# Sums of squares for the norms: transposed squares summed by VectorE in place of fp32 products with ones, with another table of turns

## The chip, the cores and the metric

The kernel runs on one core of a Trainium2 chip. The metric is the device time of one execution in microseconds; less is better. A core has five engines, each with its own instruction queue that is worked off in order: TensorE (PE; its weight loads are listed apart as PEld), VectorE (DVE), ScalarE (ACT), GpSimd (POOL) and SyncE (SP), which here issues nearly all transfers between HBM and SBUF. PE writes its results to PSUM, and the other engines read them there.

## The reference

One layer over 2048 tokens of width 1024: a normed input is multiplied by one wide weight, and its parts go to three branches (RWKV-7 with 8 heads of 64, sliding-window attention with 8 query and 2 key heads of 64, cross-attention into 256 memory tokens with 4 heads of 128), which are gated, merged and projected back. What the change touches are the norms per head, each of which needs the sum of squares of every token over the 64 or 128 channels of a head:

```python
def rms_norm(x, g):
    xf = x.astype(jnp.float32)
    y = xf * lax.rsqrt(jnp.mean(xf * xf, axis=-1, keepdims=True) + RMS_EPS)
    return (y * g.astype(jnp.float32)).astype(x.dtype)
...
kk = heads(k * k_k.astype(f32))
kk = kk / jnp.maximum(jnp.linalg.norm(kk, axis=-1, keepdims=True), L2_EPS)      # RWKV
...
q = rope(rms_norm(q.reshape(bsz, t, SW_HEADS, SW_HEAD_DIM), q_g), pos)          # window
k = rope(rms_norm(k.reshape(bsz, t, SW_KV_HEADS, SW_HEAD_DIM), k_g), pos)
...
q = rms_norm(q.reshape(bsz, t, X_HEADS, X_HEAD_DIM), xq_g)                      # cross
km = rms_norm(km.reshape(bsz, m, X_HEADS, X_HEAD_DIM), xk_g)
```

## The kernel before

**Tiling.** The tokens are worked through in four blocks of 512 (`TB`, the loop over `sb`). Activations stand channel by token: 128 partitions hold 128 channels, 512 columns hold tokens. Every large product is made from three products of split operands (`gemm3`, lines 462 to 464: high by high, low by high, high by low, in the type fp32r), 128 by 128 weights against 512 columns. These are called the dense products below. The small products (heads, transposes, chunk products of RWKV) are in plain fp32.

**Weights.** `wblock` (lines 440 to 448) fetches a weight block into the ring `whl` of nine buffers. In the first token block it loads the raw weight (443), ACT makes the high half (444), DVE the low half (445), and SP stores both halves to HBM (448). In the later blocks the stored halves are loaded (440), and neither ACT nor DVE has to do with them. A store on SP waits for line 445, and the loads behind it on SP wait with it.

**The sums of squares.** ACT squares a projection into `sq` (128 channels by 512 tokens). Since the channels stand on partitions, the sum over a head's channels is taken by PE: `tok_stat` (lines 509 to 512) multiplies, for each 128 tokens, the tile `sq` as the stationary operand with `bones` (two columns, each with ones for 64 channels) or `ones1` (one column of ones). The result, tokens by heads, is 128 by 1 or 2 numbers in PSUM per product. DVE copies the 2 to 8 columns to `st8` (lines 626, 953, 1014, 1050; in RWKV line 725 takes a maximum in place of the copy and line 726 a reciprocal). Outside RWKV, POOL raises them to the power -1/2 (`rpow`, lines 427 to 431). Where the factor has to be channel by token again, `bcast_T` has DVE widen it (523) and PE transpose it back (525).

Each token block has thirteen such sums of four tiles: one per RWKV pair of heads (723), one per cross head (951), one for the window keys (1012), one per pair of window query heads (1048). The memory keys have four of two tiles in the first block (624). In all that is 4 x 13 x 4 + 4 x 2 = 216 tile products. The PSUM tiles come from two rings of two banks, `rw` in RWKV and `as_` elsewhere.

**The order.** Within a token block the code is written as five streams, and a string of `TURNS` (one for the first block, one for the others) says which stream goes on at each turn: r for RWKV, a for both attentions, b and c for two merges, g for gates. That is the program order. `order` then lays all instructions out: `Step` gives each a cost, `lay_out` fills each engine's queue by rank, and `latest` sets the ranks anew from due times, in three passes. Each engine's queue is then fixed in that order. A change of a cost or of a turn therefore moves instructions on every engine.

Of the kernel before, what the change touches and what calls it, by code (L numbers as in the profile page):

```python
# [9 lines left out]
F32 = mybir.dt.float32  # L10
# [4 lines left out]
ALU = mybir.AluOpType  # L15
# [6 lines left out]
NRT = 6  # L22
PASSES = 3
TURNS = (
    "rararrarbaaaaaaaaaaraaaaarbaracarbaabaaarbrgrabrraaaaarabbbaaaarrraararccccgcgccrgrgrrgrrgrrgrrrrc",
    "rararaaaaraaaraaaaarbraabararaabbaraaaaacaararraabbrbgraaaaarraabbarraccrgcccgrcrgrgrgrcrgrrgrrrrc",
)
RING = 9
C = 64
# [24 lines left out]
class Step:  # L54
# [36 lines left out]
    def cost_PE(self):  # L91
        out, mov, w = self.writes[0], *self.reads[:2]
        n = self.n(out)
        self.tile = tuple(128 if r[3][0][1] > 64 else 64 if r[3][0][1] > 32 else 32 for r in (mov, out))
        self.dense = mov[5] == F32R
        if self.dense:
            self.busy = max(110, 13.5 + 0.417 * n)
        elif self.ins.is_transpose:
            self.busy = 109 if self.tile[0] == 128 else 63
        elif self.tile[1] == 128:  # L100
            self.busy = 223 + max(0, n - 128) * 1.7
        else:
            self.busy = 34 if self.tile[1] < 64 else max(58, 0.86 * n) if self.tile[0] > 64 else max(58, 0.48 * n)
        self.dur = max(270, self.busy + 160)
# [66 lines left out]
def lay_out(tc, todo):  # L171
# [50 lines left out]
    for s in todo:  # L222
        if not missing[s]:
            offer(s)
    tile, fp32, wires = (128, 128), False, 0
    for _ in todo:
        best = None
        for e, rs in ready.items():
            if rs:
                at = max(clock[e], min(rs.values()))  # L230
                if best is None or at < best[0]:
                    best = at, e
        at, e = best
        can = [s for s, t in ready[e].items() if t <= at]
        s = min(can, key=lambda s: s.rank)
        if e == "PE":
            s = min(can, key=lambda s: (fp32 and s.tile != tile, s.rank))
            if s.tile != tile:
                at += 95
            clock[e] = at + s.busy  # L240
            if s.dense and fp32:
                clock[e] += 95
            elif s.tile != tile and s.tile[1] < 128:
                clock[e] += 49
            tile, fp32 = s.tile, not s.dense
        else:
            clock[e] = at + s.busy
        s.end = at + s.dur
        if s.bytes:
            wires = s.end = max(wires, s.end) + s.bytes / 330  # L250
        del ready[e][s]
        orders[e].append(s)
        again = set()
        for name in s.opens:
            tag = source[name]
            tags[tag].free.pop(0)
            heads[tag] += 1
            again.add(tag)
        for name in {r[0] for r in s.reads + s.writes}:
            if e not in last[name] or last[name][e].end < s.end:  # L260
                last[name][e] = s
            left[name] -= 1
            if not left[name] and source[name] in tags:
                tags[source[name]].free.append(name)
                again.add(source[name])
        for a in s.after:
            missing[a] -= 1
            if not missing[a]:
                offer(a)
        if again:  # L270
            for a in [a for rs in (parked, *ready.values()) for a in rs if any(source[n] in again for n in a.opens)]:
                offer(a)
# [45 lines left out]
def build(tc, A, nsb=4):  # L318
# [27 lines left out]
    def rw_ps():  # L346
        return ps.tile([128, 512], F32, name="rw", bufs=2)

    def s_ps():
        return ps.tile([128, 512], F32, name="as_", bufs=2)  # L350
# [155 lines left out]
        return o  # L506


    def tok_stat(sq, nh, ntile, out):
        rhs = bones if nh == 2 else ones1  # L510
        for i in range(ntile):
            PE.matmul(out[:, i * nh:(i + 1) * nh], sq[:, i * 128:(i + 1) * 128], rhs, start=True, stop=True)

    bones2 = cp.tile([128, 128], F32R, name="bones2")
    V.tensor_copy(bones2.rearrange("p (a b) -> p a b", b=64), bones.unsqueeze(2).to_broadcast([128, 2, 64]))
    ones1 = cp.tile([128, 1], F32, name="ones1")
    V.memset(ones1, 1.0)

    def bcast_T(out, st, nh, ntile):

# [89 lines left out]
    def mem_kv(mT):  # L610
# [9 lines left out]
            kgs[h] = sq, kg  # L620

        def stats(h):
            st = s_ps()
            tok_stat(kgs[h][0], 1, 2, st)
            rs = xp.tile([128, 8], F32, name="st8", bufs=2)
            V.tensor_copy(rs[:, :2], st[:, :2])
            rpow(rs[:, :2], rs[:, :2], EPS, 1.0 / 128)
            sts[h] = rs

# [63 lines left out]
    def rwkv_prep(p, sb, hT, lwla, group):  # L693
# [25 lines left out]
        yield  # L719
        sq = tmp()  # L720
        S.activation(sq, k, AF.Square, scale=pcol("k_k", p))
        st = rw_ps()
        tok_stat(sq, 2, 4, st)
        rs = xp.tile([128, 8], F32, name="st8", bufs=2)
        V.tensor_scalar(rs, st[:, :8], 1e-24, None, op0=ALU.max)
        V.reciprocal(rs, rs)
        rs2 = rw_ps()
        bcast_T(rs2, rs, 2, 4)
# [209 lines left out]
    def cross_head(h, sb, hT, yh, yl):  # L938
# [8 lines left out]
        sq = g2()  # L947
        S.activation(sq, o, AF.Square)
        yield
        st = s_ps()  # L950
        tok_stat(sq, 1, 4, st)
        rs = xp.tile([128, 8], F32, name="st8", bufs=2)
        V.tensor_copy(rs[:, :4], st[:, :4])  # L953
        rpow(rs[:, :4], rs[:, :4], 128 * EPS)
        mx = xp.tile([128, 8], F32, name="mx", bufs=2)
        sps = []
# [43 lines left out]
    def swa_kv(sb, hT):  # L1000
        o = slice(sb * TB, (sb + 1) * TB)
        if sb:
            G.tensor_copy(kH[:, :, :128], kH[:, :, TB:])
            G.tensor_copy(kL[:, :, :128], kL[:, :, TB:])
            G.tensor_copy(vt[:, 0], vt[:, 4])
        kp = proj(B_SK, hT)
        sq = g2()
        S.activation(sq, kp, AF.Square)
        kg = g2()
        S.activation(kg, kp, AF.Copy, scale=pcol("k_g"))  # L1010
        st = s_ps()
        tok_stat(sq, 2, 4, st)
        rs = xp.tile([128, 8], F32, name="st8", bufs=2)
        V.tensor_copy(rs, st[:, :8])
        rpow(rs, rs, EPS, 1.0 / 64)
        yield
        bc = s_ps()
        bcast_T(bc, rs, 2, 4)
        V.tensor_tensor(kg, kg, bc, op=ALU.mult)
        rope(kg, kg)  # L1020
        for g, h in enumerate((EV, OD)):
            for to in (h, EV if g else OD):
                S.activation(kH[to, g, 128:], kg[h], AF.Copy)
                V.tensor_tensor(kL[to, g, 128:], kg[h], kH[h, g, 128:].bitcast(F32), op=ALU.subtract)
        vp = proj(B_SV, hT)
        vs = g2()
        S.activation(vs, vp, AF.Copy)
        yield
        pt = s_ps()
        for i in range(4):  # L1030
            PE.transpose(pt[:, i * 128:(i + 1) * 128], vs[:, i * 128:(i + 1) * 128], ident)
        S.activation(vt[:, 1:].rearrange("p a b -> p (a b)"), pt, AF.Copy)

    def swa_pair(j, sb, hT, yh, yl):
# [9 lines left out]
            S.activation(q[h], qg[h], AF.Copy)  # L1044
            V.tensor_tensor(q[l], qg[h], q[h].bitcast(F32), op=ALU.subtract)
        yield
        st = s_ps()
        tok_stat(sq, 2, 4, st)
        rs = xp.tile([128, 8], F32, name="st8", bufs=2)
        V.tensor_copy(rs, st[:, :8])  # L1050
        rpow(rs, rs, 64 * EPS)
        g = j // 2
        mx = xp.tile([128, 4, 4], F32, name="mxs", bufs=2)
# [233 lines left out]
```

## Time and profile before

| | |
|---|---|
| median of 3 runs | 2307.17 us (2304.47 to 2309.24) |
| the profiled execution | 2305.93 us, its span 2304.2 us |
| DVE busy | 1436.1 us, 62% of the span |
| ACT, POOL busy | 840.3 us (36%), 218.1 us (9%) |
| DMA queues | 487.84 MB moved, mean 212 GB/s |
| records of line 512 (216 fp32 products) | two each, 432 |

The span runs from the first to the last instruction of the profiled execution; what lies around it is 1.7 us. The page gives busy times by engine, the span in 40 slices, the chain of work that ended last, and groups of instructions; the trace behind it answers for single lines, waits and windows. Matmuls overlap, so the duration of one (some 0.4 us for 512 columns) is longer than the distance from one start to the next, and it is the distances that add up.

### The profile page before, as it was taken

The numbers are of one execution on the slowest core, as the hardware profiler recorded it, in microseconds if no ns is written. First come the engines' busy times: TensorE is split into PE (matmuls) and PEld (weight loads), VectorE is DVE, ScalarE is ACT, GpSimd is POOL, SyncE is SP. The second block draws the span as 40 slices with busy tenths as digits, with TensorE's granted clock in tenths as the row PEclk, the third lists the DMA queues.
The fourth block names the chain that finished last, engine by engine and source line by source line (L and its number), as shares of the span: only waits on it lengthen the run. The fifth ranks groups of instructions, "written<-read, shape, count | busy, mean of one in ns | idle before, by whom it ended". The sixth has DMA issues, their size and how long they took to land.

```text
span 2304.2 us, 38725 instructions
## 1 busy us (share of the span) xinstructions
PE 2264.8 (98%) x14304; PEld 1857.4 (81%) x14304; DVE 1436.1 (62%) x4429; ACT 840.3 (36%) x1805; POOL 218.1 (9%) x297
## 2 busy tenths in 40 slices
PE   7999999999999999999999999999999999999999
PEld 6788888867788888887888888887788888888787
DVE  6698787637457866633627686762453777765252
ACT  5465545316334253311513343421232435241030
POOL 2001001021000000101101000101200000000210
PEclk9999999999999999999999999999999999999999
DMA  7777777777865555466674555556666554556665
GB/s 240 252 259 241 257 243 253 269 238 272 310 234 185 170 161 189 162 209 242 228 251 155 191 170 166 178 171 228 223 240 221 170 173 156 177 162 206 221 214 181
DMA packets 218077, 487.84 MB, mean 212 GB/s; under 512 B 19616, under 2 KB 81440, under 8 KB 217888
## 3 DMA queue, kind: packets, MB, share of 16 engines
q1 hardware_dynamic: 205216, 462.28, 60.0%
q10 hardware_dynamic: 12672, 23.07, 2.9%
q8 instruction: 114, 1.87, 0.3%
q14 instruction: 75, 0.61, 0.1%
HBM read 357.88 MB, written 127.40 MB: 211 GB/s over the span
## 4 chain that ended last, share of the span: by engine, by line
PE 86%; DVE 5%; DMA 4%; ACT 3%; issue 1%; POOL 0%; SPq 0%; ACTq 0%; POOLq 0%; DVEq 0%
PE mm L462 20%; PE mm L463 20%; PE mm L464 20%; PE rw L763 2%; DMA whl<-in_w_in 2%; PE mm L1144 1%; PE mm L1146 1%; PE mm L1145 1%; PE oo L1099 1%; PE oo L988 1%; PE rw L871 1%; PE rw L884 1%; PE rw L879 1%; ACT g L1079 1%; DVE whl L445 1%
## 5 line engine op out<-in xcount | busy, mean ns | idle before, releaser
L462 PE MATMUL mm<-hH,whl 128*128 128x512 f32 x1888 | 749.6, 397 | 7.8 <-ACT whl L444 7.3
L463 PE MATMUL mm<-hL,whl 128*128 128x512 f32 x1888 | 748.1, 396 | 0.0
L464 PE MATMUL mm<-hH,whl 128*128 128x512 f32 x1888 | 745.0, 395 | 0.0
L462 PEld LDWEIGHTS mm<-hH,whl 128*128 128x128 f32 x1888 | 355.4, 188 | 81.6 <-ACT whl L444 8.8
L463 PEld LDWEIGHTS mm<-hL,whl 128*128 128x128 f32 x1888 | 355.5, 188 | 73.3 <-issue 0.3
L464 PEld LDWEIGHTS mm<-hH,whl 128*128 128x128 f32 x1888 | 355.4, 188 | 72.0 <-DVE whl L445 1.3
L1110 ACT ACTIVATE g<-mm 128x512 f32<-128x512 f32 x96 | 57.5, 599 | 371.2 <-PE mm L464 371.0
L445 DVE TENSOR_TENSOR whl<-whl 128x512 fp32r<-128x512 f32 x174 | 121.0, 697 | 76.6 <-ACT whl L444 67.9
L444 ACT ACTIVATE whl<-whl 128x512 fp32r<-128x512 f32 x174 | 109.2, 629 | 153.8 <-DMA whl<-in_w_in 92.1
L782 DVE TENSOR_TENSOR ibc<-ibc,Yi 128x248 f32<-128x248 f32 (+30 forms) x496 | 143.8, 290 | 11.1
L462 PE MATMUL mm<-yh,whl 128*128 128x512 f32 x384 | 149.1, 390 | 1.6 <-ACT yh L932 0.8
L781 DVE STREAM_SHUFFLE ibc<-Nc 128x248 f32<-128x248 f32 (+30 forms) x496 | 150.4, 312 | 0.1
L463 PE MATMUL mm<-yl,whl 128*128 128x512 f32 x384 | 149.1, 390 | 0.1
L464 PE MATMUL mm<-yh,whl 128*128 128x512 f32 x384 | 149.1, 389 | 0.0
L783 DVE TENSOR_TENSOR Yi<-Yi,ibc 128x248 f32<-128x248 f32 (+30 forms) x496 | 140.2, 283 | 1.0
L1125 DVE SCALAR_TENSOR_TENSOR g<-g,mm 128x512 f32<-128x512 f32 x64 | 43.7, 684 | 91.0 <-PE mm L464 90.9
L1079 ACT ACTIVATE g<-g,mxs,st 128x256 f32<-128x256 f32 (+1 forms) x128 | 74.4, 584 | 43.6 <-DVE mxs L1072 23.4
L427 POOL TENSOR_SCALAR st<-st 128x4 f32<-128x4 f32 (+1 forms) x32 | 10.4, 324 | 810.1 <-DVE st L953 411.7
L462 PEld LDWEIGHTS mm<-yh,whl 128*128 128x128 f32 x384 | 72.0, 188 | 18.2 <-DVE g L1125 2.1
L463 PEld LDWEIGHTS mm<-yl,whl 128*128 128x128 f32 x384 | 72.1, 188 | 16.3 <-DVE yl L933 1.4
L464 PEld LDWEIGHTS mm<-yh,whl 128*128 128x128 f32 x384 | 72.1, 188 | 14.8
L877 POOL TENSOR_TENSOR SP<-Z,Pl 64x256 f32<-64x256 f32 x64 | 41.6, 650 | 305.7 <-DVE Z L890 204.4
(1735 smaller groups left out, 3495.4 us busy)
## 6 DMA issues: line engine op xcount, KB each, us to landing
whl<-k SPq DMA_DIRECT2D x474, 512.0 KB, 3.4
k<-whl SPq DMA_DIRECT2D x158, 512.0 KB, 3.3
whl<-f SPq DMA_DIRECT2D x128, 256.0 KB, 4.5
whl<-in_w_in SPq DMA_DIRECT2D x118, 256.0 KB, 3.6
f<-FT SPq DMA_DIRECT2D x48, 512.0 KB, 4.6
f<-FT SPq DMA_DIRECT2D x32, 256.0 KB, 4.1
g<-in_x ACTq DMA_DIRECT2D x32, 256.0 KB, 5.4
out<-g ACTq DMA_DIRECT2D x32, 256.0 KB, 4.1
```

What stands on the lines that cost most here:

```text
L444: S.activation(w[:, 0], raw, AF.Copy)
L445: V.tensor_tensor(w[:, 1], raw, w[:, 0].bitcast(F32), op=ALU.subtract)
L462: PE.matmul(out, lh, rh, start=i == 0, stop=False)
L463: PE.matmul(out, lh, rl, start=False, stop=False)
L464: PE.matmul(out, ll, rh, start=False, stop=i == n - 1)
L763: PE.matmul(g[:, c], BK[h, c0 + c], Q[h, c0 + c], start=True, stop=True)
L781: V.stream_shuffle(bc[:, :, :n], Nc[:, :, s + 1:], [s] * 32)
L782: V.tensor_tensor(bc[:, :, :n], bc[:, :, :n], Y[:, :, s:s + 1].to_broadcast([128, NC_, n]), op=ALU.mult)
L783: V.tensor_tensor(Y[:, :, s + 1:], Y[:, :, s + 1:], bc[:, :, :n], op=ALU.add)
L1079: S.activation(prs[b][:, i, m0:], prs[b][:, i, m0:], AF.Exp, scale=r2[:, b, i:i + 1], bias=mx[:, b, i:i + 1], accum_out=mx[:, b, 2 + i:3 + i])
L1110: S.activation(t, gp, AF.Tanh, scale=0.5)
L1125: V.scalar_tensor_tensor(g, g, 1.0, pp, op0=ALU.add, op1=ALU.mult)
```

## The change

`tok_stat` no longer multiplies with ones. PE transposes each 128 by 128 tile of squares into PSUM, so that tokens stand on partitions and channels on columns, and one `tensor_reduce` of DVE sums 64 or 128 columns each from PSUM straight into `st8`. The copies out of PSUM go; in RWKV the maximum stays, now on SBUF. `ones1` goes. The planner's cost of a transpose is set to 112 ns in place of 109, and what it adds to the first dense product after fp32 work is 30 ns after transposes alone, where it was 95 after any. Both turn strings are others.

```diff
@@ TURNS (the first of two strings)
-    "rararrarbaaaaaaaaaaraaaaarbaracarbaabaaarbrgrabrraaaaarabbbaaaarrraararccccgcgccrgrgrrgrrgrrgrrrrc",
+    "rrararaaaraaabaaaaaraaabrrraaaaabacbrbgaaaararrabrbaaabraabgaaararraararcccccccrggrrgrgrrgrrrrgrrc",
@@ cost_PE
         elif self.ins.is_transpose:
-            self.busy = 109 if self.tile[0] == 128 else 63
+            self.busy = 112 if self.tile[0] == 128 else 63
@@ lay_out
             if s.dense and fp32:
-                clock[e] += 95
+                clock[e] += fp32
...
-            tile, fp32 = s.tile, not s.dense
+            tile, fp32 = s.tile, 0 if s.dense else 30 if s.ins.is_transpose and fp32 < 95 else 95
@@ build
-    def tok_stat(sq, nh, ntile, out):
-        rhs = bones if nh == 2 else ones1
+    def tok_stat(sq, nh, ntile, pt):
+        rs = xp.tile([128, 8], F32, name="st8", bufs=2)
         for i in range(ntile):
-            PE.matmul(out[:, i * nh:(i + 1) * nh], sq[:, i * 128:(i + 1) * 128], rhs, start=True, stop=True)
+            PE.transpose(pt[:, i * 128:(i + 1) * 128], sq[:, i * 128:(i + 1) * 128], ident)
+        V.tensor_reduce(rs[:, :ntile * nh], pt[:, :ntile * 128].rearrange("p (a b) -> p a b", b=128 // nh), axis=AX.X, op=ALU.add)
+        return rs
@@ rwkv_prep
-        st = rw_ps()
-        tok_stat(sq, 2, 4, st)
-        rs = xp.tile([128, 8], F32, name="st8", bufs=2)
-        V.tensor_scalar(rs, st[:, :8], 1e-24, None, op0=ALU.max)
+        rs = tok_stat(sq, 2, 4, rw_ps())
+        V.tensor_scalar(rs, rs, 1e-24, None, op0=ALU.max)
@@ cross_head (mem_kv, swa_kv and swa_pair alike)
-        st = s_ps()
-        tok_stat(sq, 1, 4, st)
-        rs = xp.tile([128, 8], F32, name="st8", bufs=2)
-        V.tensor_copy(rs[:, :4], st[:, :4])
+        rs = tok_stat(sq, 1, 4, s_ps())
```

The order of the instructions moves on all engines. Three places show how; a number behind a name tells one buffer from another, and in the changed kernel the lines stand up to 14 earlier.

**PE, the first RWKV sum of the second token block.** Before, the four products with ones (L512, into `rw_6952`) stand between dense products, and seven dense products follow until the transposes of `bcast_T` (L525):

```order
L462 MATMUL mm_6915<-hH_6319,whl_6918 128x512
L463 MATMUL mm_6915<-hL_6320,whl_6918 128x512
L464 MATMUL mm_6915<-hH_6319,whl_6918 128x512
L512 MATMUL rw_6952<-c_bones_118,rt_6950 128x2 x4
L462 MATMUL mm_6981<-hH_6319,whl_6982 128x512
L463 MATMUL mm_6981<-hL_6320,whl_6982 128x512
```

In the changed kernel the transposes of the squares stand among those of a cross head (L976), with that head's products (L980) and three dense ones between them and L525:

```order
L976 MATMUL as__7099<-c_ident_96,g2_6926 128x128 x3
L512 MATMUL rw_6990<-c_ident_96,rt_6988 128x128 x4
L976 MATMUL as__7099<-c_ident_96,g2_6926 128x128
L976 MATMUL as__7110<-c_ident_96,g2_6929 128x128 x4
L462 MATMUL mm_7247<-hH_6321,whl_7248 128x512
L463 MATMUL mm_7247<-hL_6322,whl_7248 128x512
L464 MATMUL mm_7247<-hH_6321,whl_7248 128x512
L980 MATMUL oo_7098<-g2_7106,vm_6862 128x256 x2
L980 MATMUL oo_7098<-g2_7117,vm_6862 128x256 x2
L525 MATMUL rw_6999<-c_ident_96,rt_7000 128x128 x4
```

The sum has moved next to other transposes, and its work is now one of a row of transposes.

**PE, the sum for the window keys in the second token block** (L512 into `as__8061` before, `as__7979` now). Before, eleven more dense products follow the last row shown until the transposes L525 into `as__8196`:

```order
L462 MATMUL mm_8217<-hH_6319,whl_8218 128x512
L463 MATMUL mm_8217<-hL_6320,whl_8218 128x512
L512 MATMUL as__8061<-c_bones_118,g2_8057 128x2 x4
L464 MATMUL mm_8217<-hH_6319,whl_8218 128x512
L462 MATMUL mm_8217<-hH_6319,whl_8218 128x512
```

In the changed kernel chunk products of RWKV (L758, line 763 before) stand on both sides, and after the last row shown eight more dense products follow until L525 into `as__7988`:

```order
L758 MATMUL rw_8045<-FT_165 128x128 x4
L758 MATMUL rw_8046<-FT_165 128x128 x4
L512 MATMUL as__7979<-c_ident_96,g2_7975 128x128 x4
L462 MATMUL mm_8212<-hH_6321,whl_8213 128x512
L758 MATMUL rw_8057<-FT_165 128x128 x4
L758 MATMUL rw_8058<-FT_165 128x128 x4
L463 MATMUL mm_8212<-hL_6322,whl_8213 128x512
L464 MATMUL mm_8212<-hH_6321,whl_8213 128x512
```

So between sum and L525 stood 13 dense products, and now stand eleven and eight chunk products.

**DVE, the same place.** Before, the copy of the sums (L1014), one step of the rope tables (L559) and the widening copy (L523) follow each other:

```order
L556 CAST g2_7968<-g2_7974 128x512
L558 SCALAR_TENSOR_TENSOR g2_7963<-g2_7968,g2_7963 128x512 x4
L1014 COPY st8_8066<-as__8061 128x8
L559 TENSOR_SCALAR g2_7963<-g2_7963 128x512
L523 COPY rt_8197<-st8_8066 128x512
```

In the changed kernel the reduction (L513) stands where the copy stood, and four operations, two of them on the chunk products (L760), stand between it and the widening copy:

```order
L513 TENSOR_REDUCE st8_7980<-as__7979 128x8
L558 SCALAR_TENSOR_TENSOR g2_7847<-g2_7852,g2_7847 128x512
L760 TENSOR_TENSOR FT_165<-rw_8057,gmask_124 128x4x128
L558 SCALAR_TENSOR_TENSOR g2_7847<-g2_7852,g2_7847 128x512
L760 TENSOR_TENSOR FT_165<-rw_8058,gmask_124 128x4x128
L523 COPY rt_7989<-st8_7980 128x512
```

So four operations stand between sum and widening where there was one.

More of the change, by code (lines that the diff above doesn't have):

```diff
@@ L24 @@
 TURNS = (
-    "rararrarbaaaaaaaaaaraaaaarbaracarbaabaaarbrgrabrraaaaarabbbaaaarrraararccccgcgccrgrgrrgrrgrrgrrrrc",
-    "rararaaaaraaaraaaaarbraabararaabbaraaaaacaararraabbrbgraaaaarraabbarraccrgcccgrcrgrgrgrcrgrrgrrrrc",
+    "rrararaaaraaabaaaaaraaabrrraaaaabacbrbgaaaararrabrbaaabraabgaaararraararcccccccrggrrgrgrrgrrrrgrrc",
+    "aarrbraraaaaraaaaaaaraaaraararbgbaaabracararabaaarrbbabraaaabararaarrgracgcccccrgrgrcrgrrgrrrrrrgc",
 )
@@ L224, in lay_out @@
             offer(s)
-    tile, fp32, wires = (128, 128), False, 0
+    tile, fp32, wires = (128, 128), 0, 0
     for _ in todo:
@@ L506, in proj @@
         return o
-    def tok_stat(sq, nh, ntile, out):
-        rhs = bones if nh == 2 else ones1
+    def tok_stat(sq, nh, ntile, pt):
+        rs = xp.tile([128, 8], F32, name="st8", bufs=2)
         for i in range(ntile):
-            PE.matmul(out[:, i * nh:(i + 1) * nh], sq[:, i * 128:(i + 1) * 128], rhs, start=True, stop=True)
+            PE.transpose(pt[:, i * 128:(i + 1) * 128], sq[:, i * 128:(i + 1) * 128], ident)
+        V.tensor_reduce(rs[:, :ntile * nh], pt[:, :ntile * 128].rearrange("p (a b) -> p a b", b=128 // nh), axis=AX.X, op=ALU.add)
+        return rs
     bones2 = cp.tile([128, 128], F32R, name="bones2")
     V.tensor_copy(bones2.rearrange("p (a b) -> p a b", b=64), bones.unsqueeze(2).to_broadcast([128, 2, 64]))
-    ones1 = cp.tile([128, 1], F32, name="ones1")
-    V.memset(ones1, 1.0)
     def bcast_T(out, st, nh, ntile):
@@ L622, in stats @@
         def stats(h):
-            st = s_ps()
-            tok_stat(kgs[h][0], 1, 2, st)
-            rs = xp.tile([128, 8], F32, name="st8", bufs=2)
-            V.tensor_copy(rs[:, :2], st[:, :2])
+            rs = tok_stat(kgs[h][0], 1, 2, s_ps())
             rpow(rs[:, :2], rs[:, :2], EPS, 1.0 / 128)
@@ L949, in cross_head @@
         yield
-        st = s_ps()
-        tok_stat(sq, 1, 4, st)
-        rs = xp.tile([128, 8], F32, name="st8", bufs=2)
-        V.tensor_copy(rs[:, :4], st[:, :4])
+        rs = tok_stat(sq, 1, 4, s_ps())
         rpow(rs[:, :4], rs[:, :4], 128 * EPS)
@@ L1010, in swa_kv @@
         S.activation(kg, kp, AF.Copy, scale=pcol("k_g"))
[L1011 to L1014, printed above, removed]
+        rs = tok_stat(sq, 2, 4, s_ps())
         rpow(rs, rs, EPS, 1.0 / 64)
@@ L1046, in swa_pair @@
         yield
[L1047 to L1050, printed above, removed]
+        rs = tok_stat(sq, 2, 4, s_ps())
         rpow(rs, rs, 64 * EPS)
```

## The prediction, made before the run

> **What bounds the kernel now.** I read the page first (busy time, clock, chain), then PE's waits, then the stretches.
>
> ```profile
> PE 2264.8 (98%) x14304; PEld 1857.4 (81%) x14304; DVE 1436.1 (62%) x4429; ACT 840.3 (36%) x1805; POOL 218.1 (9%) x297
> PEclk9999999999999999999999999999999999999999
> PE 86%; DVE 5%; DMA 4%; ACT 3%; issue 1%; POOL 0%; SPq 0%; ACTq 0%; POOLq 0%; DVEq 0%
> L462 PE MATMUL mm<-hH,whl 128*128 128x512 f32 x1888 | 749.6, 397 | 7.8 <-ACT whl L444 7.3
> ```
>
> PE is busy in 98% of the span, the granted clock is near full in every slice, and 86% of the chain that ended last is PE. The dense products wait 7.8 us in all at the first of their three lines. What PE waits for:
>
> ```profile
> PE rw L496 <- DVE g L491: 10.5, 2, 10.0
> PE mm L462 <- ACT whl L444: 8.2, 5, 2.1
> PE mm L1144 <- ACT whl L444: 3.4, 3, 2.8
> PE as__18920 L525 <- DVE rt L523: 1.4, 1, 1.4
> PE as__8196 L525 <- DVE rt L523: 1.4, 1, 1.4
> PE as__13558 L525 <- DVE rt L523: 1.4, 1, 1.4
> ...
> 0.00:640.00 640.00, 610.80 (x3756) 494.08 (x3757) 457.49 (x1309) 306.53 (x634) 69.43 (x97) 0.99 0.76 258
> 640.00:1200.00 560.00, 557.74 (x3550) 459.32 (x3549) 330.84 (x1053) 184.19 (x406) 50.85 (x69) 1.00 0.60 201
> ```
>
> The columns of a wait are the sum, the times and the longest, in us; those of a stretch are its length, then PE, PEld, DVE, ACT and POOL busy, the clock, the DMA share and GB/s. The largest wait (10.0) is the start. Three of 1.4 hang on the sums for the window keys. The first token block (0 to 640) has 29.2 us without PE work, the second 2.3 us of 560. So in three blocks of four, a microsecond less on PE is a microsecond less of time, as long as the work around it keeps up; in the first the weights, which ACT and DVE must split there, are nearly as tight.
>
> **The products with ones go, transposes come.** Both can be read as excursions from dense work, from the dense start ahead to the second dense start behind:
>
> ```profile
> 167.33 0.39 PE L463 MATMUL mm<-hL,whl 128*128 128x512 f32 x1
> 167.56 0.95 PE L512 MATMUL as__1908<-c_bones,g 128*128 128x2 f32 x8
> 168.36 0.49 PE L464 MATMUL mm<-hH,whl 128*128 128x512 f32 x1
> 168.69 0.40 PE L462 MATMUL mm<-hH,whl 128*128 128x512 f32 x1
> ...
> 771.21 0.39 PE L464 MATMUL mm<-hH,whl 128*128 128x512 f32 x1
> 771.44 0.60 PE L1031 MATMUL as__8248<-c_ident,g 128*128 128x128 f32 x4
> 771.79 0.47 PE L462 MATMUL mm<-hH,whl 128*128 128x512 f32 x1
> 772.10 0.39 PE L463 MATMUL mm<-hL,whl 128*128 128x512 f32 x1
> ```
>
> A dense start follows another after 0.23 us (167.33 to 167.56). Four tiles times ones: 168.69 - 167.33 = 1.36, less two dense at 0.23, is **0.90 us**. Four fp32 transposes of the same shape and kind, already in the kernel: 772.10 - 771.21 = 0.89, less 0.46, is **0.43 us**. The product needs two records per tile (x8 for four tiles), the transpose one (x4). So each sum of four tiles gives 0.47 us back. There are 52 of these and four of half the size, 54 in full ones: 54 x 0.47 = **25.4 us** off PE. Both durations hold the slower first dense product behind (0.31 to 0.33 in place of 0.23).
>
> **The order.** Counted over PE's queue, the dense work falls into 336 runs before and 358 now. A further run is at most a further first dense product at 0.31 (771.79 to 772.10) in place of 0.23: 22 x 0.08 = **+1.8 us**; the least is nothing, since a run split by work that stood elsewhere among small products costs nothing new. I take the 1.8.
>
> **The reduction on DVE.** The nearest rows are a reduction of the same size from PSUM, one from SBUF, and what goes:
>
> ```profile
> L962 DVE TENSOR_REDUCE mx<-as__938 x1: 685/685/685, 83.8 to 83.8; 128x2 f32<-128x512 f32 x1
> L904 DVE TENSOR_REDUCE var<-rt 128x8 f32<-128x512 f32 x16 | 11.0, 685 | 11.8 <-ACT rt L902 11.7
> L725 DVE TENSOR_SCALAR st<-rw 128x8 f32<-128x8 f32 x16 | 2.6, 161 | 12.3 <-PE rw L512 12.3
> L1014 DVE COPY st<-as__8061 x1: 168/168/168, 763.7 to 763.7; 128x8 f32<-128x8 f32 x1
> ```
>
> PSUM or SBUF, 2 or 8 results, it is 0.685 us. Outside RWKV it stands in for a copy of 0.16 (36 times +0.53 us); in RWKV it is wholly new, as the maximum stays (16 times +0.69); the four halves add some 0.25 each (an estimate from half the columns). DVE: 19.1 + 11.0 + 1.0 = +31 us, 1436 to about 1467, 64% of the span. I cost this at nothing as work, since PE's dense products hide it: in the second block DVE works 331 us of 560. Where a sum's result is awaited it is a delay, though. Queued behind the reduction on DVE are the rest of its own chain and whatever the order put there, low weight halves (line 445) in the first block among it.
>
> **The chain of the window keys** is where that shows, since PE waits there already:
>
> ```profile
> 763.72 0.17 DVE L1014 COPY st<-as__8061 128x8 f32<-128x8 f32 x1
> 764.36 1.64 POOL L431 TENSOR_TENSOR st<-st,mhalf 128x8 f32<-128x8 f32 x1
> 765.96 1.90 POOL L770 TENSOR_TENSOR FT<-FT,Pl 128x1024 f32<-128x1024 f32 x1
> 766.03 2.11 DVE L523 COPY rt<-st 128x512 f32<-128x512 f32 x1 [1.81 <-POOL st L431]
> 768.19 0.66 PE L525 MATMUL as__8196<-c_ident,rt 128*128 128x128 f32 x4 [1.40 <-DVE rt L523]
> ...
> L523 DVE COPY rt<-st x24: 286/427/2108, 36.2 to 2036.2; 128x512 f32<-128x512 f32 x20, 128x256 f32<-128x256 f32 x4
> ...
> 91.28 1.64 PE rw L763 x16
> ```
>
> The widening copy takes 0.43 us at its median and 2.11 here, beside a POOL operation that started 0.07 us ahead and ended 0.28 us ahead of it. From the copy's start to PE's transposes are 4.47 us. In the changed order POOL's two operations still follow one another, so I keep the 2.11; the longer reduction makes it 5.0. The cover was 13 dense products (13 x 0.23 = 3.0); it is now eleven and eight chunk products (2.5 + 1.64 = 4.2, the 1.64 from sixteen records, two a product). The wait of 1.4 comes to 4.47 + 0.53 - 4.2 + 0.1 = 0.9: three times -0.5 = **-1.5 us**. The ends are -4.2 (the waits go, if POOL and DVE miss each other) and +1.6 (the cover doesn't count, the reduction shows in full).
>
> **The other sums.** In RWKV the chain from sum to transposes is 0.69 us longer; before, PE waited at none of these sixteen places. In the second block three dense products, eight products of a cross head and its transposes now stand there, where seven dense did. Below is nothing, above 16 x 0.69 = 11 us; nearest is the trace with no wait, so I take a tenth of a microsecond each, **+1.6 us**.
>
> **The sum:** -25.4 + 1.8 - 1.5 + 1.6 = -23.5 us. The profiled execution took 2305.93, which gives 2282.4; it stood 1.2 under the median of the three, so the forecast is **2283.6**. The setup of one column of ones on DVE goes too, at no price, ahead of PE's first work.
>
> **A rule against the change.** For a transpose the profile shows a duration longer than for a product with ones:
>
> ```profile
> L525 PE MATMUL rw<-c_ident,rt x64: 270/273/328, 75.6 to 2037.1; 128*128 128x128 f32 x64
> L512 PE MATMUL rw<-c_bones,rt x128: 165/251/272, 70.5 to 2035.5; 128*128 128x2 f32 x128
> ```
>
> The Trainium skill, "TensorE: Matmul & The Clock Gate", "Part 4: PE-mode transpose", says the same from another side: a 128 by 128 transpose takes about 275 ns in a kernel (measured there in bf16), and doesn't count as work that keeps PE's clock up. By that price 216 of them would be some 59 us, and the change a loss. The trace has the 273 ns as a latency: four transposes from 771.44 make the next dense product start at 771.79. It shows no loss of clock in the stretch of 640 to 1200 (1.00), which is full of them.
>
> **The rivals.**
> *A. The first block keeps its time.* There the low halves stand on DVE, and the stores behind them on SP:
>
> ```profile
> SPq L448 <- DVE whl L445: 193.6, 92, 6.0
> 476.00:486.00 10.00, 7.94 (x81) 5.63 (x80) 2.13 (x5) 1.86 (x3) 0.45 (x2) 0.85 0.78 259
> ```
>
> SP waits 193.6 us for line 445 before stores, with loads behind it. DVE's extra there is 9 x 0.53 + 4 x 0.69 + 1.0 = 8.5 us. If each of these microseconds delays weights that PE awaits, the time is 2283.6 + 8.5 = **2292**; a wait of 2 us, as at 481, also halves the clock for a while (0.85 over those ten us), which can add some 2 to 5 more. Against it: from 70 to 450, where all these sums stand, PE waited for no weights.
> *B. The other turns also remove waits.* PE's waits behind the start come to some 23 us. With half of them gone: 2283.6 - 11 = **2272**. For it: they hang on order alone; against it, most hang on loads, which the change doesn't touch.
> *C. The reduction stands in PE's way everywhere: slower.* If PE finds no other work between the transposes of the squares and what needs the sum, DVE's 31 us become PE's: 2283.6 + 31 - 1.6 = **2313**. It decides from about three quarters of the places (23.5 of 31). For it, the three waits of the keys; against it, these are the only ones that L523 ends, in 20 places of four tiles.
> *D. Transposes don't stream:* 216 x 0.273 = 59.0 in place of 54 x 0.90 = 48.6 us, +10.4, with the other terms **2319**. The starts 0.1 us apart speak against it.
> *E. The transposes of the squares don't come out as one pass* but as two records each: nothing is saved on PE, and 1.9 is lost, **2309**. Against it: 64 calls, 64 records in the row of L525.
>
> **How the numbers follow.** The forecast has 0.62 (its own range 2279 to 2290), A 0.18, B 0.10, C 0.04, D 0.02, E 0.04. A measurement of this kernel tells apart about 0.2%, 4.6 us. Faster by more: 0.62 + 0.18 + 0.10 = 0.90; the same: E, 0.04; slower: C and D, 0.06. The range goes from within B to the slow end of A, **2274 to 2297**; C, D, E and the tails of A and B, some 0.16, are outside.
>
> **What would show it.** Line 512 with 216 records for 216 tiles, four of them between dense starts at 0.43 us more; PE's busy time at 2264.8 - 23.6, near 2241; a reduction of 0.685 on line 513, and DVE near 1467; waits at L525 of about 0.9 in three blocks; PE without work in the first block near 29 us still. Transposes further apart than 0.11 us, or new waits of PE for line 513 or 523 at many places, would make the prediction wrong; so would more waits for line 444.

## The result, and the profile after

| | before | changed |
|---|---|---|
| median, us | 2306.03 (4 runs, 2304.47 to 2309.24) | 2277.66 (4 runs, 2276.01 to 2280.36) |
| ratio, 95% interval | | 0.9876 [0.9859, 0.9893] |
| profiled execution, its span | 2305.93, 2304.2 | 2280.36, 2278.6 |

The change takes 28.4 us off the median (25.6 off the spans of the two profiled executions; the changed one is the longest of its four). The forecast was 2283.6, a gain of 23.5. The page of the changed kernel, its engines, the shares of the chain that ended last, and the first of its groups:

```profile
PE 2236.3 (98%) x14088; PEld 1824.9 (80%) x14088; DVE 1468.4 (64%) x4444; ACT 835.2 (37%) x1803; POOL 212.3 (9%) x297
PE 87%; DMA 5%; DVE 5%; ACT 2%; issue 1%; SPq 0%; POOL 0%; ACTq 0%; DVEq 0%
L462 PE MATMUL mm<-hH,whl 128*128 128x512 f32 x1888 | 749.1, 397 | 7.5 <-ACT whl L444 5.6
```

PE has 216 records fewer (14304 less 14088: one for each of the 216 tiles) and 28.5 us less busy time; DVE has 32.3 more. The single operations are what the nearest rows said. Line 512 by itself in the changed kernel (ns: least, median, most), then the group of line 513, then a piece of the timeline:

```profile
L512 PE MATMUL rw<-c_ident,rt x64: 270/272/328, 67.7 to 2027.8; 128*128 128x128 f32 x64
```

```profile
L513 DVE TENSOR_REDUCE st<-rw 128x8 f32<-128x512 f32 x16 | 10.9, 683 | 11.1 <-PE rw L512 10.9
```

```profile
314.24 0.40 PE L464 MATMUL mm<-hH,whl 128*128 128x512 f32 x1
314.48 0.60 PE L512 MATMUL as__3717<-c_ident,g 128*128 128x128 f32 x4
314.83 0.31 PE L1049 MATMUL as__3729<-KsH,g 128*128 128x128 f32 x1
```

64 transposes have 64 records; a reduction takes 0.683 us; and four transposes hold PE from 314.48 to the next start at 314.83. The windows below are cut at the ends of the first two token blocks, each at the end of the block's last output product (the columns as in the prediction's windows). Before:

```profile
0.00:633.90 633.90, 604.70 (x3729) 489.03 (x3730) 456.32 (x1308) 305.92 (x633) 69.43 (x97) 0.99 0.76 258
633.90:1191.20 557.30, 555.04 (x3538) 457.09 (x3537) 330.03 (x1050) 182.52 (x402) 50.85 (x69) 1.00 0.60 202
```

The changed kernel:

```profile
0.00:622.90 622.90, 593.90 (x3669) 477.97 (x3670) 464.12 (x1311) 304.00 (x631) 65.86 (x97) 0.99 0.77 261
622.90:1175.20 552.30, 548.94 (x3486) 450.18 (x3485) 338.01 (x1055) 181.26 (x402) 50.00 (x69) 1.00 0.61 205
```

In the second block PE is busy 6.1 us less (555.04 to 548.94), which is 13 sums at 0.47, as forecast. But its idle time grows from 2.3 to 3.4 us, and the block is only 5.0 shorter. The first block, where 15 sums at 0.47 should give 7.0, is 11.0 shorter. The third and fourth, cut in the same way, are 4.6 and 4.3 shorter. So the later blocks gave less than the sums, and the first more.

Part of that is the clock. In some stretches of 3.4 us the trace grants PE half of it: four in the first block before, two in the changed kernel. One of each (before, then changed; the clock is the third number from the end):

```profile
483.00:486.40 3.40, 3.40 (x23) 2.34 (x22) 0.64 (x2) 0.63 (x1) 0.00 (x0) 0.50 0.36 145
487.70:491.10 3.40, 3.40 (x23) 2.53 (x22) 1.54 (x3) 0.63 (x1) 0.85 (x1) 0.50 0.35 142
```

PE does half a stretch's work in it, so two fewer are worth 3.4 of the 11.0 us; with the 7.0 of the sums, 0.6 is left. Their number differs between executions. The mean granted clock is 0.996 to 0.997 in the repeats of before and 0.998 in those of the change, which is 2 to 4 of the 28 us.

PE's waits in the changed kernel:

```profile
PE rw L496 <- DVE g L491: 10.5, 3, 9.5
PE mm L462 <- ACT whl L444: 5.9, 4, 2.8
PE mm L1130 <- ACT whl L444: 3.3, 3, 2.2
PE as__13354 L525 <- DVE rt L523: 1.4, 1, 1.4
PE as__18720 L525 <- DVE rt L523: 1.4, 1, 1.4
PE as__7988 L525 <- DVE rt L523: 1.4, 1, 1.4
PE as__7360 L976 <- DVE g L974: 1.3, 1, 1.3
PE as__12726 L976 <- DVE g L974: 1.3, 1, 1.3
PE as__18092 L976 <- DVE g L974: 1.3, 1, 1.3
```

The three waits for the window keys are still 1.4 (forecast 0.9), and three of 1.3 behind the softmax of a cross head are new. The timeline of the first of the key sums:

```profile
744.27 0.66 PE L512 MATMUL as__7979<-c_ident,g 128*128 128x128 f32 x4
745.42 0.68 DVE L513 TENSOR_REDUCE st<-as__7979 128x8 f32<-128x512 f32 x1
746.29 0.47 POOL L429 TENSOR_SCALAR st<-st 128x8 f32<-128x8 f32 x1 [36.08 <-DVE st L513]
746.84 1.64 POOL L431 TENSOR_TENSOR st<-st,mhalf 128x8 f32<-128x8 f32 x1
748.45 1.89 POOL L765 TENSOR_TENSOR FT<-FT,Pl 128x1024 f32<-128x1024 f32 x1
748.51 2.11 DVE L523 COPY rt<-st 128x512 f32<-128x512 f32 x1
750.68 0.65 PE L525 MATMUL as__7988<-c_ident,rt 128*128 128x128 f32 x4 [1.36 <-DVE rt L523]
```

The copy L523 again takes 2.11 us beside POOL. From the reduction's start to PE's transposes are 5.26 us (the prediction had 5.0); PE ran dry at 750.68 - 1.36 = 749.32, so its work covered 3.90 of them (the prediction had 4.1).

### The profile page after: what moved, and what is told of

Same layout as the page of the kernel before. It is cut to its first block, busy times and chain, and to the rows that moved or that the text cites. A ratio compares the mean times of both kernels' runs of the same rounds, so it can differ in the third digit from the quotient of the medians.

```text
span 2278.6 us, 38340 instructions
## 1 busy us (share of the span) xinstructions
PE 2236.3 (98%) x14088; PEld 1824.9 (80%) x14088; DVE 1468.4 (64%) x4444; ACT 835.2 (37%) x1803; POOL 212.3 (9%) x297
## 4 chain that ended last, share of the span: by engine, by line
PE 87%; DMA 5%; DVE 5%; ACT 2%; issue 1%; SPq 0%; POOL 0%; ACTq 0%; DVEq 0%
PE mm L462 21%; PE mm L463 21%; PE mm L464 21%; PE rw L758 2%; DMA whl<-in_w_in 2%; PE oo L1085 1%; PE mm L1131 1%; PE mm L1130 1%; PE mm L1132 1%; PE oo L980 1%; DMA whl<-k 1%; DMA rt<-in_x 1%; PE rw L879 1%; PE rw L866 1%; DVE whl L445 1%; PE rw L874 1%
## 5 line engine op out<-in xcount | busy, mean ns | idle before, releaser
L777 DVE TENSOR_TENSOR ibc<-ibc,Yi 128x248 f32<-128x248 f32 (+30 forms) x496 | 143.7, 290 | 11.1
L1144 DVE SCALAR_TENSOR_TENSOR g<-mm,g 128x512 f32<-128x512 f32 x16 | 11.0, 690 | 83.4 <-PE mm L1132 78.0
```

What stands on the lines that cost most here:

```text
L777: V.tensor_tensor(bc[:, :, :n], bc[:, :, :n], Y[:, :, s:s + 1].to_broadcast([128, NC_, n]), op=ALU.mult)
```

## The experiments

Two theories. **The forecast's:** the sums save PE 0.47 us each in any order, the order costs little, and DVE's reduction is hidden by dense products. **The rival:** the reduction does stand in PE's way (rival C), and it is the order that hides it; then the same code in the old order gains nothing, and the order has a worth of its own. All ratios come from five rounds against before; a ratio is turned into time as (ratio - 1) x 2306.

| run | what | median | ratio [95%] | us |
|---|---|---|---|---|
| e1 | new sums, turns and costs of before | 2310.22 | 1.0027 [1.0016, 1.0038] | +6.2 |
| e2 | new turns alone | 2312.07 | 1.0035 [1.0022, 1.0048] | +8.1 |
| e10 | new planner costs alone | 2320.05 | 1.0064 [1.0052, 1.0076] | +14.8 |
| e4 | new sums and costs, old turns | 2308.04 | 1.0015 [1.0004, 1.0026] | +3.5 |
| e3 | new sums and turns, old costs | 2295.18 | 0.9962 [0.9948, 0.9975] | -8.8 |
| e11 | the changed kernel again | 2277.44 | 0.9878 [0.9865, 0.9891] | -28.1 |
| e8 | new sums, before's order held | 2318.52 | 1.0043 [1.0030, 1.0055] | +9.9 |
| e12 | as e8, without the reduction | 2289.89 | 0.9935 [0.9922, 0.9947] | -15.0 |
| e9 | old sums, the new order held | 2298.94 | 0.9957 [0.9941, 0.9972] | -9.9 |
| e6 | the change, its order held, reduction twice as long | 2311.06 | 1.0010 [0.9999, 1.0021] | +2.3 |
| e7 | the change, its order held, key widening on ACT | 2286.49 | 0.9900 [0.9887, 0.9914] | -23.1 |
| e5 | the change, each square transposed twice | 2302.66 | 0.9995 [0.9987, 1.0003] | -1.2 |

### One part of the change at a time

e1 takes the changed kernel back to the old turns and the old planner costs; e2 gives before the new turns; e4 is the changed kernel with the old turns. From the changed kernel to e1:

```diff
-    "rrararaaaraaabaaaaaraaabrrraaaaabacbrbgaaaararrabrbaaabraabgaaararraararcccccccrggrrgrgrrgrrrrgrrc",
+    "rararrarbaaaaaaaaaaraaaaarbaracarbaabaaarbrgrabrraaaaarabbbaaaarrraararccccgcgccrgrgrrgrrgrrgrrrrc",
...
-            self.busy = 112 if self.tile[0] == 128 else 63
+            self.busy = 109 if self.tile[0] == 128 else 63
...
-                clock[e] += fp32
+                clock[e] += 95
```

> The sums by transposes, with the old turns and the old costs of the planner. If the gain is PE time saved per sum (54 x 0.47 us), it is there without the new turns: 2306 - 25 + 2 = 2283 us, within 5. If the gain comes mostly from the new turns, this is 2295 to 2306. If the longer reduction needs the new turns to be hidden, it shows here as waits of PE behind lines 513 and 523 at more places than the three of the window keys, and the time is between.

> The old sums with the new turns alone. If the gain is PE time saved per sum, nothing of it is here: 2306 us, give or take the 5 that another order can be worth. If the new turns carry it, 2280 to 2290. The measured 28 us off is 5 more than the 23.5 forecast; if the turns give these 5, this run is near 2301, and its trace has fewer dips of the clock in the first block (four before, two after the change).

> The sums by transposes and the new costs, with the old turns. Beside the run with the old costs too it shows what the costs (112 in place of 109, 30 in place of 95) do to the order: within 3 us of that run if they matter little. Beside the whole change it shows what the turns give: 0 to 5 us slower than 2278 if PE time carries the gain, 15 or more if the turns do.

None of the three is faster than before. PE's waits in e1 for the high weight halves, and its row of the clock:

```profile
PE mm L462 <- ACT whl L444: 8.0, 7, 2.6
PE mm L1130 <- ACT whl L444: 6.3, 5, 2.7
```

```profile
core 0: 2306.3 us, clock 0.994
```

In e1 the second to fourth block take 553.8, 553.8 and 549.8 us, 8.4 less in sum than before, where 39 sums at 0.47 should give 18.3. The first takes 645.0, 11.1 more than before, with 39.7 idle (29.2 before): the waits for weights are 14.3 (11.6 before, 9.2 in the change), and the clock drops more (0.994; 0.997 before). Over all executions of e1 the mean clock is 0.003 lower than before's, some 7 us, as much as the whole loss of 6.2. So the new sums alone are no gain, and with the clock set aside they are level with before.

The new turns alone are a loss, and not by the clock: e2 has one stretch at half clock in the first block where before has four, which its expectation tied to a gain. Its first block is 2.3 shorter, but the later ones are 2.6, 3.2 and 3.8 longer; why isn't shown.

### The costs of the planner

e10 gives before the new planner costs, by the edit below; e3 takes the same edit back in the changed kernel. e11 has no edit; it repeats the changed kernel beside them.

```diff
-            self.busy = 109 if self.tile[0] == 128 else 63
+            self.busy = 112 if self.tile[0] == 128 else 63
...
-                clock[e] += 95
+                clock[e] += fp32
...
-            tile, fp32 = s.tile, not s.dense
+            tile, fp32 = s.tile, 0 if s.dense else 30 if s.ins.is_transpose and fp32 < 95 else 95
```

> The whole change with the old costs in the planner, and so another order from the same code and the same turns. If turns, costs and code only fit together, so that any other order loses what was fitted: 2285 to 2310, with more waits of PE in the first block. If orders of the planner are worth about the same: within 4 us of 2278.

> The kernel before with the new costs in the planner, code and turns as they were. If its order was fitted to its turns as well: 2310 to 2320. If orders of the planner are worth about the same: within 4 us of 2306.

> The whole change once more, on the same chip as the three above, so that they can be set beside it: 2278 us, 0.9876 of before, within 0.002.

The costs are numbers in the planner; no instruction is another. They give 19.3 us in one kernel (-8.8 to -28.1) and lose 14.8 in the other; with the new sums and the old turns they move 2.7 (e1 and e4). Some 4 to 6 us of the 19.3 and the 14.8 go through the clock, whose mean is 0.9956 in both e3 and e10, against 0.998 in the change and 0.997 before. So sums, turns and costs fit one another, and no share of the gain can be given to one of them. Five orders of the new sums (e1, e3, e4, e8, the change) reach from 0.9876 to 1.0043 of before's time.

### The new sums in the old order, with the reduction and without

To part the order from the work, the planner is told for each exchanged instruction the duration of the one that it stands in for. Every engine's queue then stands as in the kernel whose order is held, by the traces (in e8 three small copies on DVE have changed places with a neighbour). e8 has the new sums in before's order:

```diff
+        if ins.name in PLAN:
+            self.dur, self.busy = PLAN[ins.name]
...
+            t = PE.transpose(pt[:, i * 128:(i + 1) * 128], sq[:, i * 128:(i + 1) * 128], ident)
+            PLAN[t.ins.name] = 383, 223
+        t = V.tensor_reduce(rs[:, :ntile * nh], pt[:, :ntile * 128].rearrange("p (a b) -> p a b", b=128 // nh), axis=AX.X, op=ALU.add)
+        c = 155 + 1.05 * ntile * nh
+        PLAN[t.ins.name] = c, max(60, c - 85)
```

> The sums by transposes in the order of before: the planner is given the costs of the old instructions for the new ones, so that every engine's queue stands as it did (336 dense runs). If each sum saves PE 0.47 us and the order is what ate it in the run with the code alone, PE's work falls by 25 us and the time by 15 to 25, to 2281 to 2291, less what the longer reduction holds up where the order left no room for it. If the longer reduction is what ate it, this order too gives nothing: 2300 to 2310, with new waits of PE behind lines 513 and 523.

e12 is e8 with the summation left out: in place of the reduction DVE copies 2 to 8 columns of the transposed squares (in RWKV it takes their maximum with a constant), as short as before.

```diff
-        t = V.tensor_reduce(rs[:, :ntile * nh], pt[:, :ntile * 128].rearrange("p (a b) -> p a b", b=128 // nh), axis=AX.X, op=ALU.add)
+        if low:
+            V.tensor_scalar(rs[:, :n], pt[:, :n], low, None, op0=ALU.max)
+        else:
+            V.tensor_copy(rs[:, :n], pt[:, :n])
```

> The order of before, the squares transposed, and the old copies of 2 to 8 columns behind them: the summation is left out (in RWKV the maximum is taken with 1e12, so that the state stays finite), and DVE does what it did before. If PE's saving of 0.47 us per sum is real in that order and the longer reduction ate it (2318 with it), this is 2306 - 25 = 2281 us, within 5, and PE's waits are those of before. If the order itself cannot use a shorter sum, it is near 2306.

The engines on the page of e8 and its second block:

```profile
PE 2253.1 (97%) x14088; PEld 1825.9 (79%) x14088; DVE 1464.2 (63%) x4444; ACT 839.4 (36%) x1805; POOL 216.9 (9%) x297
...
633.90:1194.30 560.40, 552.63 (x3486) 450.48 (x3486) 336.83 (x1055) 181.83 (x402) 50.65 (x69) 1.00 0.62 202
```

The same two rows of e12:

```profile
PE 2244.4 (98%) x14088; PEld 1824.4 (80%) x14088; DVE 1434.2 (63%) x4428; ACT 839.1 (37%) x1805; POOL 217.0 (9%) x297
...
625.40:1180.00 554.60, 551.34 (x3486) 450.79 (x3486) 329.55 (x1051) 181.90 (x402) 50.79 (x69) 1.00 0.62 204
```

PE's waits in e8, where line 533 holds the transposes of `bcast_T` (525), 531 the widening copy (523), 519 the reduction and 1058 a product of a window head:

```profile
PE rw L533 <- DVE rt L531: 9.4, 12, 1.6
...
PE as__13566 L533 <- DVE rt L531: 2.3, 1, 2.3
...
PE as__2423 L1058 <- DVE st L519: 1.6, 1, 1.6
...
PE as__945 L467 <- DVE st L519: 0.8, 1, 0.8
```

In before's order the change is a loss. PE waits twelve times behind RWKV's sums, 9.4 us in all, where before it waited at none; the waits for the keys are 2.3. The last row stands once in each block: a score product of a cross head (467 is 462) waits for the reduction, although it reads nothing of the sum. It writes the PSUM tile that the reduction still reads, since the ring `as_` has two.

e12 differs from e8 by DVE's work alone: DVE is busy 1434.2 us in e12 and 1464.2 in e8, and the times differ by 9.9 + 15.0 = 24.9. So of 30.0 us more work on DVE 24.9 are PE's time in that order: rival C. Some 2 of them go through the clock (in mean 0.9976 in e8 and 0.9984 in e12).

Since the order is one, the starts of PE's matmuls can be set side by side. From e12 to e8 the starts at 49 places where PE waits for DVE lie 21.1 us further apart (a place is counted where the distance to the start ahead grew by over 0.04 us), while some 13 400 other starts move by less than that each, and by 0.03 us in all. So it is the waits, and not a PE that is slowed everywhere while DVE reads PSUM.

Without the reduction the sums should give 25.4, and e12 gives 15.0. The sums do give it. Where one stands between dense products, the stretch that the prediction priced at 0.90 us for products and 0.43 for transposes has a median of 0.90 before and 0.44 in e8, in e12 and in the change; over all sums the starts are 23.4 us closer in e12 than before. But PE then comes to its other waits earlier, and the chains on DVE are no shorter: at 46 places the starts lie 13.2 us further apart than before, of which 8.2 show as idle. One of these places, again a score product that waits for the tile (before, then e12, where 467 and 468 are 462 and 463):

```profile
659.71 0.40 PE L463 MATMUL mm<-hL,whl 128*128 128x512 f32 x1
659.95 0.28 PE L462 MATMUL as__7039<-km,g 128*128 128x256 f32 x1
...
650.89 0.40 PE L468 MATMUL mm<-hL,whl 128*128 128x512 f32 x1
651.59 0.39 PE L467 MATMUL as__7037<-km,g 128*128 128x256 f32 x1 [0.30 <-DVE st L523]
```

The start is 0.70 us behind the dense one in place of 0.24, and of these 0.46 the trace shows 0.30 as idle: the dense product shows 0.40, though the next could start after 0.24. The first 0.16 of the wait shows as busy.

### The order by itself, and its margin

e9 puts the products with ones and the copies back into the changed kernel and holds its order (in RWKV a copy stands ahead of the maximum):

```diff
-            PE.transpose(pt[:, i * 128:(i + 1) * 128], sq[:, i * 128:(i + 1) * 128], ident)
+            t = PE.matmul(st[:, i * nh:(i + 1) * nh], sq[:, i * 128:(i + 1) * 128], rhs, start=True, stop=True)
+            PLAN[t.ins.name] = 272, 112
...
+        t = V.tensor_copy(rs[:, :ntile * nh], st[:, :ntile * nh])
+        PLAN[t.ins.name] = 155 + 1.05 * ntile * 128, 70 + 1.05 * ntile * 128
```

> The old products with ones, followed by the copy, in the order of the whole change (the planner is given the new costs for the old instructions; in RWKV copy and maximum are both done, 0.16 us more on DVE than before). If the saving is 0.47 us on PE per sum, this is the whole change plus 25: 2303 us, and so within 5 of before; the order by itself is then worth what is left. If the order of the change carries more than the sums, it is near 2290.

Its first two blocks:

```profile
0.00:628.40 628.40, 601.10 (x3729) 486.84 (x3730) 459.62 (x1312) 305.43 (x631) 65.37 (x97) 0.99 0.76 259
628.40:1185.40 557.00, 555.45 (x3538) 457.93 (x3537) 332.05 (x1054) 181.68 (x402) 50.62 (x69) 1.00 0.62 203
```

Its longest waits at the places where the change waits 1.3 and 1.4 (line 988 is 976, 537 is 525):

```profile
PE as__7362 L988 <- DVE g L986: 0.6, 1, 0.6
...
PE as__18722 L537 <- DVE rt L535: 0.3, 1, 0.3
```

The order alone is worth 9.9 us (by the interval 6.5 to 13.6); of the 7.2 by which its span is shorter, 5.5 are in the first block (633.9 to 628.4; 1.7 of it by the clock, which is at half for 10.2 us in place of 13.7), and the second is equal within 0.3, although it holds 3.4 us at half clock, worth 1.7, that before has not. The sums then give -28.6 + 9.9 = -18.7 in this order, in each block (first 628.4 to 622.9, second 557.0 to 552.3, of which 1.7 is that stretch). Against 25.4 on PE, 6.7 are given back, and the waits show most of them: the three for the keys grow from at most 0.3 to 1.4, the three at line 976 from 0.6 to 1.3, together some 5.7. Set side by side as above, the starts of the change against those of e9 give -23.9 at the sums, +7.3 at waits for DVE, +2.6 at waits for ACT and -2.0 where one of the two runs at half clock.

e6 holds the changed order and has the reduction read its columns twice, into 16 results of which 8 are used:

```diff
+        twice = pt[:, :ntile * 128].rearrange("p (a b) -> p a b", b=128 // nh).unsqueeze(1).to_broadcast([128, 2, n, 128 // nh])
+        t = V.tensor_reduce(rs[:, :2 * n].rearrange("p (t a) -> p t a", t=2), twice, axis=AX.X, op=ALU.add)
+        PLAN[t.ins.name] = 155 + 1.05 * ntile * 128, 70 + 1.05 * ntile * 128
```

> The whole change, its order kept on every engine, with each reduction reading its columns twice and giving twice as many results, of which the first half is used: 0.68 us more on DVE 52 times, some 35 us, and as much more delay in each chain behind a sum. If DVE's work is hidden by PE's: 2278 + 3 x 0.7 for the keys + up to 5 elsewhere = 2278 to 2285. If it stands in PE's way everywhere: 2313.

The group of its reduction, and then two of PE's waits (533 is 525 again):

```profile
L520 DVE TENSOR_REDUCE st<-rw 128x16 f32<-128x1024 f32 x16 | 19.5, 1216 | 10.9 <-PE rw L517 10.9
```

```profile
PE as__13354 L533 <- DVE rt L531: 2.0, 1, 2.0
PE rw L533 <- DVE rt L531: 1.5, 5, 0.4
```

The forecast's theory falls here. 54 x (1.216 - 0.683) = 28.8 us more of DVE cost 2.3 + 28.6 = 30.9. The new order hides the reduction that it was planned for, and little beyond it. Only a part shows as idle (the keys 2.0 in place of 1.4, five of RWKV 1.5 in all); by the starts, waits for DVE cost 18.9 us more, of which 11.7 show. Another part goes through the clock (0.993 over the span, 0.999 in the change). In the second and in the fourth block it is at half for 3.4 us right behind the wait of 2.0 for the keys, in the third, behind the same wait, it isn't; the second:

```profile
765.30:768.70 3.40, 3.40 (x9) 2.65 (x8) 3.29 (x7) 2.77 (x4) 0.00 (x0) 0.50 0.64 204
```

These two stretches are 3.4 of the 20.8 us by which the second to fourth block are longer; the other 17.4 are 0.45 for each of 39 sums, where the reduction is 0.53 longer. In the first block, 10.4 longer, 23.9 us at half clock in place of 6.8 account for 8.5.

### The copy beside POOL

e7 holds the changed order and has ACT widen the factors of the window keys.

```diff
-        V.tensor_copy(rep.rearrange("p (a b) -> p a b", b=w), st[:, :ntile * nh].unsqueeze(2).to_broadcast([128, ntile * nh, w]))
+        to, from_ = rep.rearrange("p (a b) -> p a b", b=w), st[:, :ntile * nh].unsqueeze(2).to_broadcast([128, ntile * nh, w])
+        if act:
+            MOVED.add(S.activation(to, from_, AF.Copy).ins.name)
```

> The whole change, its order kept, with the widening copy of the window keys' factors (line 523, four times) on ACT in place of DVE. If the copy takes 2.11 us there because a POOL operation runs beside it on DVE, ACT does it in some 0.7 us, the three waits of PE of 1.4 us at the transposes behind it go, and the time falls by 3 to 4 us, to 2274. If the copy is slow for another reason (its input arrives late, the form is slow), the waits stay and so does the time.

The timeline of the same place in e7 (778 is 765, 534 the widening, 538 is 525):

```profile
750.75 2.42 POOL L778 TENSOR_TENSOR FT<-FT,Pl 128x1024 f32<-128x1024 f32 x1
750.82 0.63 ACT L534 ACTIVATE rt<-st 128x512 f32<-128x512 f32 x1 [4.32 <-POOL st L440]
751.44 2.00 DVE L572 TENSOR_SCALAR g<-g 128x512 f32<-128x512 f32 x1
751.50 0.66 PE L538 MATMUL as__7988<-c_ident,rt 128*128 128x128 f32 x4
```

The widening takes 0.63 us on ACT and PE's wait is gone, but the next operation of DVE now takes 2.00. No time is won: -23.1 against the change's -28.6, so 5.5 are lost, and where isn't shown. It is POOL's operation, not the copy, that makes the 2.11.

### Do transposes stream?

e5 transposes each tile of squares twice into the same place (the order is planned anew):

```diff
-        for i in range(ntile):
+        for i in [*range(ntile)] * 2:
```

> The whole change with each tile of squares transposed twice into the same place (the second writes the same numbers), 216 transposes more. If the time follows PE and a transpose costs 0.11 us there: 2278 + 216 x 0.11 = 2302 us, within 4. If transposes do not stream and cost 0.27 each: 2336. If PE had slack at these places: near 2278.

The engines on its page, and the row of its clock:

```profile
PE 2260.3 (98%) x14304; PEld 1845.0 (80%) x14304; DVE 1467.3 (64%) x4444; ACT 836.2 (36%) x1803; POOL 212.9 (9%) x297
```

```profile
core 0: 2297.8 us, clock 0.999
```

216 further transposes (x14304) cost 2302.66 - 2277.66 = 25.0 us by the medians and 28.6 - 1.2 = 27.4 by the ratios, 0.12 to 0.13 each, and the clock stays. Rival D is out. The Trainium skill's price of about 275 ns for each transpose ("TensorE: Matmul & The Clock Gate", "Part 4: PE-mode transpose") would be an estimate of 59 us; the runs show some 270 ns as a latency, with 0.12 to 0.13 us from one transpose to the next, and no loss of clock.

## Why the prediction was right, and where only the sum was

**The sums, -25.4: right.** One record for a tile, 13 x 0.47 = 6.1 us less PE work in the second block, 0.12 to 0.13 a transpose in e5, and 0.44 in place of 0.90 us at a sum between dense products, in the old order as in the new.

**The reduction on DVE, "I cost this at nothing as work, since PE's dense products hide it": this step failed.** DVE's 64% of the span says nothing about it. Each reduction lies on the way from a square to a transpose that PE needs soon, or holds a PSUM tile that PE writes next, and its length is PE's wait unless the order has put enough work between. In the old order 24.9 of 30.0 us on DVE reach PE (e8 against e12). In the new order the sums give back 6.7 in place of the 0.1 that the steps of the keys and of RWKV had together.

**The order, +1.8: wrong in sign and in size.** I counted runs of dense products (336 to 358) and priced a run. e9 has the same runs and the old sums, and is 9.9 us faster than before. So the count of runs gave neither the sign nor the size. 5.5 us are in the first block, 1.7 of them by the clock; which of the many short waits there it removes isn't settled, since PE's busy time falls with them (604.70 to 601.10).

**The window keys, -1.5: wrong.** The waits stayed at 1.4. The chain is 0.26 longer than I had it, and the cover 0.2 shorter. With the old sums in the same order the waits are 0 to 0.3 (e9), so it is the new sums that hold them up.

**The other sums, +1.6: a little high in this order, far too low in the old one.** In the changed kernel no wait of RWKV at line 525 shows; in e8 they are 9.4 us, 0.6 for each of the sixteen, near the upper bound of 0.69.

**The rivals.** A (the first block keeps its time) fell: it gave 11.0, about 3.4 of it by the clock, for which the sum had no term. B, that the order gains, was right, but not by removing half of PE's waits: those listed are of much the same size, and the largest, at the start, is 10.5 as before. C's mechanism is real and came short in this order alone: e1, e3 and e4, whose orders were planned with the reduction too, gain 8.8 us at most. I held against it that "these are the only ones that L523 ends", which a profile of short sums can't say of long ones. D and E fell.

**The sum.** The order gave 9.9 where +1.8 was written, 11.7 better; the waits behind the reduction took 6.7 where 0.1 was written, 6.6 worse: -23.5 - 11.7 + 6.6 = -28.6, the measured gain. It closes by construction, since the 6.7 is what was left of the 25.4. The forecast came near by luck: two errors of opposite sign nearly cancelled. No run here beats the change.

## What to carry to other kernels

Work that leaves the busiest engine for one with room is only free if the chain through it has slack at each place: the engine's share of busy time doesn't tell that, the distance from an operation to the one that needs its result does. Where a planner sets the order, time new code in an order that is planned for it, and in more than one, and hold the order by giving the planner the old durations when the code itself is to be judged. A change of the planner's costs alone can move the time more than the edit (here +14.8 and -19.3 us), so a single timing of an edit that replans is no verdict on the edit.

## What the runs showed of the hardware

**DVE is held up beside a large POOL operation.** The copy of 0.43 us took 2.11 and ended 748.51 + 2.11 - 748.45 - 1.89 = 0.28 us after POOL's operation; in e7 another operation of DVE took 2.00 and ended 0.27 after it. The Trainium skill says that DVE and GpSimd share a pair of SBUF ports as an exclusive lock for a whole instruction, on DVE's side when its operation runs in a two-port mode or has two inputs in SBUF ("SBUF — State Buffer", "SBUF: two separate sides"). These rows, fp32 operations with one input, agree that the one that starts second ends only after the first; which ports they use isn't shown by any run here.

**PE can lose time and look busy.** In the second block e12 and e8 issue the same matmuls (x3486) in the same order at a clock of 1.00, and PE's busy time is 551.34 and 552.63 us; in the change, in another order, it is 548.94. Over the whole of e12, 13.2 us more of waiting for DVE than before show as 8.2 of idle time, since some 0.16 us of a wait behind a dense product counts as busy. So a busy share of 98% is no proof that PE lacks nothing.

**The granted clock drops for stretches of 3.4 us.** In e6 it is 0.50 from 765.3 to 768.7, and dense starts that were 0.23 us apart are 0.43 apart there. Two such stretches stand right behind a wait of 2.0 us, and a third wait of the same length has none.
